# Window attention scores from stacked operand halves, in a two-layer hybrid backbone kernel

## Chip, cores and metric

The kernel runs on one core of a Trainium2 chip. The metric is the device time of one execution in microseconds (us), lower is better; the median of 3 runs is quoted.

## What is computed

The reference is a two-layer backbone over 256 context tokens and 256 latent tokens (width 1024). Each layer mixes tokens with three branches, a state space model (s5), latent attention (MLA) and windowed attention with a sink, merges them with gates and an output projection, and then runs a 16-expert feed-forward (MoE). The part that matters here is the windowed branch: 8 query heads and 2 key heads of 64 channels.

```python
def axial_rope(x, row, col):            # cos, sin from row and column angles
    x1, x2 = x[..., : d // 2], x[..., d // 2:]
    return jnp.concatenate([x1 * cos - x2 * sin, x1 * sin + x2 * cos], axis=-1)

def window_branch(qc, kc, vc, ql, kl, vl, sink, row, col, update_ctx):
    ...
    qb = axial_rope(q, row, col).reshape(B, nb, BLOCK, WIN_KV_HEADS, WIN_GROUP, WIN_HEAD_DIM)
    k_rot = axial_rope(kl.reshape(B, L, WIN_KV_HEADS, WIN_HEAD_DIM), row, col)
    ...
    s_band = jnp.einsum('bnqkgd,bnskd->bnkgqs', qb, kb).astype(jnp.float32) * WIN_SCALE
    s_band = jnp.where(valid[None, :, None, None], s_band, NEG_INF)
    s_ctx = jnp.einsum('bnqkgd,bskd->bnkgqs', qpb, kc).astype(jnp.float32) * WIN_SCALE
    p = jax.nn.softmax(jnp.concatenate([s_band, s_ctx, sk], axis=-1), axis=-1)
```

Latent queries attend to rotated latent keys within 128 positions and, without rotation, to all context keys. In layer 0 context queries attend to context keys as well.

## The kernel before

Products that need float32 accuracy are done in float32r, a format that TensorE takes in one pass. A value is split in two float32r parts, high (the rounded value) and low (the rest). `put` (L433) makes both, with one ScalarE copy for the high part and one VectorE subtraction for the low one. `mm3` (L438) multiplies two such pairs in three passes: high by high, high by low, low by high. A product of plain float32 operands is one call of `mm` too, and shows as two matmul records in the trace.

`win_proj` (L1230) makes the operands of the windowed branch. First come the keys of both heads (projection, `rope` of the latent half, parts into KW), then four query tiles f, each with two heads on 128 rows: 24 passes of projection, `put` of the plain queries into QP, and `rope` into QR. `rope` (L1240) swaps the halves of each head with a permutation matmul (`permr`), multiplies by cosine and sine on VectorE (L1249, L1250), adds on GpSimd (L1251) and splits the result with `put`. The key's permutation is in plain float32, the queries' in two float32r passes over the parts.

`win_branch` (L1278) then walks over four head pairs hp and two query tiles qt. For each of the two heads a, one PSUM tile `sc` takes three passes with the context keys (L1297), three with the latent keys (L1299) and the mask as one pass with the identity (L1302). The operands stand on the 64 rows of one head, so each of these passes uses 64 of TensorE's 128 rows; only the mask uses 128. That is six passes and a mask per softmax row block, 16 such groups in a layer. In layer 0 there are eight more groups, of context queries on context keys: six passes and no mask (L1312). `softmax` (L1051) reads the tile on VectorE and ScalarE, `attend` (L1077) transposes the weights and multiplies them with the values. `sc` has two PSUM buffers.

Between the groups `tick` (L203) issues filler work: the branch projection of the s5 branch (`branches`, passes of F<-extra,wc over 128 rows), and in layer 0 also the modulation products (`ada_group`, records ad<-arena,silu_c, which use 32 columns of the array at a time). A scheduler sets the final order of each engine. Names in the profile: sc<-big,big and sc<-big are the score passes, sc<-round is the mask, F and mm are projections, wc are split weights, tp are transposes.

Of the kernel before, what the change touches and what calls it, by code (L numbers as in the profile page):

```python
# [7 lines left out]
F32 = mybir.dt.float32  # L8
# [37 lines left out]
def _constants():  # L46
# [28 lines left out]
    _ROUND.append(np.concatenate([pm, np.where(k <= q, 0.0, big)], 1).astype(np.float32))  # L75
# [86 lines left out]
class Net:  # L162
# [1067 lines left out]
    def win_proj(self, l, h, full):  # L1230
# [5 lines left out]
        parts = lambda i, o, f, n: self.bg[i][:, o:o + 2 * f * n].rearrange("p (f r n) -> p f r n", f=f, r=2)  # L1236
        QP, QR, KW = parts(0, 0, 4, NQ), parts(1, 0, 4, 256), parts(1, 2048, 2, 512)
        kf = self.buf("wkf", 512)

        def rope(dst, src, two=None):  # L1240
            pp = self.ps("sc")
            if two is None:
                self.mm(pp[:, :256], self.permr.bitcast(F32), src, True, True)
            else:
                for r in range(2):
                    self.mm(pp[:, :256], self.permr, two[:, r], r == 0, r == 1)
# [4 lines left out]
            nc.gpsimd.tensor_tensor(dst if two is None else t1, t1, t2, op=OP.add)  # L1251
            if two is not None:
                self.put(dst, t1)
# [9 lines left out]
        rope(kf[:, 256:512], kp[:, 256:512])  # L1263
        for kv in range(2):
            own, other = [slice(64 * a, 64 * a + 64) for a in (kv, 1 - kv)]
            self.put(KW[own, kv], kf[own])
            self.copy(KW[other, kv], KW[own, kv].bitcast(F32), "a" if kv else "v")
        for f in range(4):
# [4 lines left out]
            self.put(QP[:, f], pt[:, q0:])  # L1273
            rope(QR[:, f], pt[:, 256:], QP[:, f, :, 256 - q0:])
# [3 lines left out]
    def win_branch(self, l, Z, QP, QR, KW, full, tick):  # L1278
# [6 lines left out]
        two = lambda t, c: (t[:, 0, c], t[:, 1, c])  # L1285
        pv = lambda t: t.rearrange("p (a n) -> p a n", a=2)
        for hp in range(4):
# [3 lines left out]
            for qt in range(2):  # L1291
# [435 lines left out]
    def build(self, layers=(0, 1), stop=None):  # L1727
# [3 lines left out]
        with tc.tile_pool(name="main", bufs=1) as main, \  # L1731
# [11 lines left out]
            self.round = main.tile([128, 384], F32R, name="round")  # L1743
# [282 lines left out]
```

## Time and profile before

| what | us |
|---|---|
| median of 3 runs | 2080.92 (2080.52 to 2082.33) |
| the profiled execution | 2081.91 |
| its span | 2080.1 |
| TensorE matmul busy | 1800.9 (87%) |
| VectorE busy | 1030.1 (50%) |
| ScalarE busy | 603.5 (29%) |
| GpSimd busy | 444.6 (21%) |

The window stage runs twice: projection at about 282 to 310 us and branch at 310 to 400 us in layer 0, and 1386 to 1401 and 1401 to 1456 us in layer 1. A record of a matmul has a duration that includes its way through the array, so neighbours overlap in time; what a pass takes is read from the distance between starts. "Busy" of TensorE is therefore near full wherever passes follow each other, also where each starts late.

### The profile page before, as it was taken

To read this page: it belongs to the slowest core of one execution; us is meant where nothing else is said; L and a number is where in the kernel's file an instruction comes from. 1 tells how busy PE (TensorE), PEld (TensorE's weight loads), DVE (VectorE), ACT (ScalarE), POOL (GpSimd) and SP (SyncE) were. 2 spreads that over 40 slices of the span, in tenths; PEclk is the share of its full clock that TensorE was granted. 3 is DMA by queue.
4 is the path that set the end of the run, shared out by engine and by line. 5 is a ranking of instruction groups with operands and counts; after the bars stand their busy time and mean duration, and the time that the engine had idled before them with its cause. 6 is when DMAs were issued, how large, how long until landed. Compare 5 with 4: busy or idle time off the path is not lost.

```text
span 2080.1 us, 31699 instructions
## 1 busy us (share of the span) xinstructions
PE 1800.9 (87%) x12421; PEld 1116.5 (54%) x12421; DVE 1030.1 (50%) x2433; ACT 603.5 (29%) x1354; POOL 444.6 (21%) x590
## 2 busy tenths in 40 slices
PE   7898999999998699999799979999998876676665
PEld 5866566677776534334233358887886532232222
DVE  6867656656537712323465276977767321010102
ACT  3354343444433321000111075354553100000000
POOL 4745420011135100001334034640114000000000
PEclk9999999999999899999999989998999887686867
DMA  9256736222237689999999813541367799999996
GB/s 348 80 158 226 245 120 200 92 71 72 63 132 264 262 332 421 421 422 415 417 415 349 335 47 99 155 121 51 103 216 301 282 421 421 421 421 422 420 421 279
DMA packets 173013, 543.88 MB, mean 261 GB/s; under 512 B 18752, under 2 KB 101952, under 8 KB 122688
## 3 DMA queue, kind: packets, MB, share of 16 engines
q1 hardware_dynamic: 172864, 541.86, 68.4%
q8 instruction: 98, 1.61, 0.3%
q14 instruction: 51, 0.42, 0.1%
HBM read 540.77 MB, written 1.05 MB: 260 GB/s over the span
## 4 chain that ended last, share of the span: by engine, by line
PE 55%; DMA 25%; DVE 14%; issue 2%; ACT 2%; POOL 2%; SPq 0%; POOLq 0%; DVEq 0%; ACTq 0%
PE sc L247 17%; PE mm L247 16%; PE F L247 13%; DMA arena<-in_w_down 5%; PE ad L247 4%; PE tp L250 4%; DMA arena<-in_w_up 4%; DMA arena<-in_w_gate 3%; DVE wc L431 2%; DVE arena L572 2%; DMA big<-in_w_gate 2%; DMA h<-in_w_gate 2%; DMA arena<-in_w_in 2%; DMA arena<-in_w_ada 2%; DVE arena L885 1%
## 5 line engine op out<-in xcount | busy, mean ns | idle before, releaser
L247 PE MATMUL F<-h,wc 128*128 128x256 f32 (+1 forms) x1200 | 233.3, 345 | 2.0 <-DVE wc L431 2.0
L247 PE MATMUL sc<-arena,xs 128*32 128x256 f32 (+1 forms) x1336 | 190.4, 528 | 40.1 <-DMA arena<-in_w_up 23.3
L428 ACT ACTIVATE wc<-arena 128x512 fp32r<-128x512 f32 (+2 forms) x280 | 170.6, 619 | 180.6 <-PE F L247 63.7
L250 PE MATMUL tp<-const,arena 128*128 128x128 f32 (+2 forms) x815 | 141.7, 297 | 79.1 <-DVE arena L291 12.2
L247 PEld LDWEIGHTS F<-h,wc 128*128 128x128 f32 x1200 | 185.8, 191 | 33.2 <-issue 6.2
L247 PE MATMUL mm<-arena 128*32 128x256 f32 (+5 forms) x1244 | 186.8, 462 | 17.3 <-DMA arena<-in_w_down 10.0
L431 DVE TENSOR_TENSOR wc<-arena,wc 128x512 fp32r<-128x512 f32 (+2 forms) x205 | 158.9, 787 | 84.6 <-ACT wc L428 84.0
L431 POOL TENSOR_TENSOR wc<-arena,wc 128x512 fp32r<-128x512 f32 (+2 forms) x75 | 98.1, 1307 | 382.6 <-ACT wc L428 340.3
L1678 DVE TENSOR_TENSOR arena<-mm,arena 32x512 f32<-32x512 f32 (+1 forms) x128 | 70.9, 554 | 217.4 <-PE mm L247 215.9
L250 PEld LDWEIGHTS tp<-const,arena 128*128 128x128 f32 (+2 forms) x815 | 97.8, 149 | 145.0 <-issue 35.6
L242 ACT ACTIVATE arena<-tp 128x512 f32<-128x512 f32 (+3 forms) x142 | 62.1, 463 | 346.3 <-PE tp L250 301.9
L247 PEld LDWEIGHTS sc<-arena,xs 128*32 128x32 f32 (+1 forms) x1336 | 61.1, 132 | 144.7 <-issue 76.7
L247 PEld LDWEIGHTS mm<-arena 128*32 128x32 f32 (+2 forms) x1244 | 76.8, 137 | 102.0 <-issue 51.9
L247 PE MATMUL sc<-h,xs 128*32 128x256 f32 (+1 forms) x752 | 110.8, 526 | 19.9 <-DMA h<-in_w_gate 11.2
L264 POOL TENSOR_TENSOR lnq<-lnq,k 128x1 f32<-128x1 f32 x22 | 14.4, 658 | 501.4 <-DVE lnq L311 471.1
L1655 DVE TENSOR_TENSOR arena<-arena,sc 128x512 f32<-128x512 f32 (+1 forms) x32 | 17.8, 555 | 181.3 <-PE sc L247 181.0
L247 PE MATMUL sc<-big,xs 128*32 128x256 f32 (+1 forms) x632 | 86.0, 525 | 23.8 <-DMA big<-in_w_up 12.7
L1653 ACT ACTIVATE arena<-sc 128x512 f32<-128x512 f32 (+1 forms) x32 | 15.7, 491 | 290.9 <-PE sc L247 290.9
L247 PE MATMUL mm<-wc,h 128*128 128x512 f32 (+2 forms) x288 | 81.3, 406 | 6.2 <-DVE wc L431 2.8
L247 PE MATMUL F<-extra,wc 128*128 128x256 f32 (+1 forms) x432 | 83.4, 337 | 3.1 <-DVE smst L1060 2.1
L1654 DVE SCALAR_TENSOR_TENSOR arena<-arena,sc 128x512 f32<-128x512 f32 (+1 forms) x32 | 17.7, 554 | 135.3 <-ACT arena L1653 135.2
L247 PEld LDWEIGHTS sc<-h,xs 128*32 128x32 f32 (+1 forms) x752 | 36.7, 132 | 87.2 <-issue 60.5
(366 smaller groups left out, 3165.4 us busy)
## 6 DMA issues: line engine op xcount, KB each, us to landing
arena<-in_w_up SPq DMA_DIRECT2D x65, 1024.0 KB, 16.6
arena<-in_w_down SPq DMA_DIRECT2D x61, 1024.0 KB, 19.8
arena<-in_w_gate SPq DMA_DIRECT2D x48, 1024.0 KB, 19.5
h<-in_w_gate SPq DMA_DIRECT2D x41, 1024.0 KB, 13.9
arena<-in_w_ada SPq DMA_DIRECT2D x80, 512.0 KB, 5.8
arena<-in_w_in SPq DMA_DIRECT2D x66, 512.0 KB, 3.9
big<-in_w_up SPq DMA_DIRECT2D x26, 1024.0 KB, 19.8
h<-in_w_down SPq DMA_DIRECT2D x26, 1024.0 KB, 18.5
```

The costliest lines, as they stand in the source:

```text
L242: self.nc.scalar.activation(out, in_, AF.Copy)
L247: return self.nc.tensor.matmul(out, lhsT, rhs, start=start, stop=stop, skip_group_check=True)
L250: self.nc.tensor.transpose(out, in_, self.c("idn")[:n, :n])
L264: self.nc.gpsimd.tensor_tensor(out, in_, e.to_broadcast(list(in_.shape)), op=OP.pow)
L428: nc.scalar.activation(hi, src, AF.Copy)
L431: eng.tensor_tensor(lo, src, hi.bitcast(F32), op=OP.subtract)
L572: tt = lambda o, a, b, op: keep[0](v.tensor_tensor(o, a, b, op=op))
L885: v.tensor_tensor_scan(z, rb, z, 0.0, op0=OP.mult, op1=OP.add)
L1653: nc.scalar.activation(th, gu[0][:, :NF], AF.Tanh, scale=0.5)
L1654: v.scalar_tensor_tensor(th, th, 1.0, gu[0][:, :NF], op0=OP.add, op1=OP.mult)
L1655: v.tensor_tensor(th, th, gu[1][:, :NF], op=OP.mult)
L1678: v.tensor_tensor(YS[n][o:o + 32, c * NF:(c + 1) * NF], yp[r:r + 32, :NF], m5[r:r + 32], op=OP.mult)
```

## The change

The scores take two passes per product in place of three. The first, high by high, is as before over the 64 rows of the head. The second is over all 128 rows: for the queries of head a the high part stands on the head's own 64 rows and the low part on the other 64, and the keys are laid out the other way round, so that one pass adds high by low and low by high.

- `put_heads` replaces `put` for queries: for each of the two heads one ScalarE copy and one VectorE subtraction over 64 rows, the latter with its result on the other 64 rows.
- KW is laid out so that the copy to the other head's rows reverses the parts (same number of operations).
- `rope` can no longer use split parts. The permutation is done in plain float32, on each 64-row half by itself (64x64 products), for keys and queries. A ScalarE copy brings the query tile from PSUM to `kp` first. `permr` is a 64-column constant.

```diff
+        def put_heads(dst, src):
+            for a in range(2):
+                nc.scalar.activation(dst[rows[a], a], src[rows[a]], AF.Copy)
+                v.tensor_tensor(dst[rows[1 - a], a], src[rows[a]], dst[rows[a], a].bitcast(F32), op=OP.subtract)
...
-        def rope(dst, src, two=None):
+        def rope(dst, src, two=True):
             pp = self.ps("sc")
-            if two is None:
-                self.mm(pp[:, :256], self.permr.bitcast(F32), src, True, True)
-            else:
-                for r in range(2):
-                    self.mm(pp[:, :256], self.permr, two[:, r], r == 0, r == 1)
+            for r in rows:
+                self.mm(pp[r, :256], self.permr[r].bitcast(F32), src[r], True, True)
...
-            if two is not None:
-                self.put(dst, t1)
+            if two:
+                put_heads(dst, t1)
...
-            self.put(KW[own, kv], kf[own])
-            self.copy(KW[other, kv], KW[own, kv].bitcast(F32), "a" if kv else "v")
+            hi, lo = KW[own, kv, 1 - kv], KW[own, kv, kv]
+            nc.scalar.activation(hi, kf[own], AF.Copy)
+            v.tensor_tensor(lo, kf[own], hi.bitcast(F32), op=OP.subtract)
+            self.copy(KW[other, kv], KW[own, kv, ::-1].bitcast(F32), "a" if kv else "v")
...
-            self.put(QP[:, f], pt[:, q0:])
-            rope(QR[:, f], pt[:, 256:], QP[:, f, :, 256 - q0:])
+            put_heads(QP[:, f], pt[:, q0:])
+            self.copy(kp[:, 0:256], pt[:, 256:], "a")
+            rope(QR[:, f], kp[:, 0:256])
...
+        def score(out, q, k, a, qc, kc, stop):
+            self.mm(out, q[rows[a], a, qc], k[rows[a], 1 - a, kc], True, False)
+            self.mm(out, q[:, a, qc], k[:, a, kc], False, stop)
...
-                    self.mm3(sc[a][:, 0:256], two(QP[rows[a], hp], qc), two(KW[rows[a], kv], slice(0, 256)), True, True)
+                    score(sc[a][:, 0:256], QP[:, hp], KW[:, kv], a, qc, slice(0, 256), True)
...
-                    self.mm3(sc[a][:, 256:512], two(QR[rows[a], hp], qs), two(KW[rows[a], kv], slice(256, 512)),
-                             True, False)
+                    score(sc[a][:, 256:512], QR[:, hp], KW[:, kv], a, qs, slice(256, 512), False)
...
-                        self.mm3(sc[a][:, qt], two(QP[rows[a], hp], slice(qt * 128, qt * 128 + 128)),
-                                 two(KW[rows[a], kv], slice(0, 256)), True, True)
+                        score(sc[a][:, qt], QP[:, hp], KW[:, kv], a, slice(qt * 128, qt * 128 + 128), slice(0, 256), True)
```

TensorE's order in the first score groups of layer 0. The number after a name tells the tile apart; each sc is the score tile of one head, the size is output rows by columns. Before:

```order
L247 MATMUL sc_2718<-big_2418,big_2417 128x256 x3
L247 MATMUL sc_2718<-big_2418 128x256 x3
L247 MATMUL sc_2718<-round 128x128
L247 MATMUL sc_2794<-big_2418,big_2417 128x256 x3
L247 MATMUL sc_2794<-big_2418 128x256 x3
L247 MATMUL sc_2794<-round 128x128
L247 MATMUL ad_2396<-arena,silu_c 32x256
```

The same groups on TensorE in the changed kernel:

```order
L247 MATMUL sc_2739<-big_2418,big_2417 128x256 x2
L247 MATMUL sc_2739<-big_2418 128x256 x2
L247 MATMUL sc_2739<-round 128x128
L247 MATMUL ad_2396<-arena,silu_c 32x256 x4
L247 MATMUL sc_2811<-big_2418,big_2417 128x256 x2
L247 MATMUL sc_2811<-big_2418 128x256 x2
L247 MATMUL sc_2811<-round 128x128
L247 MATMUL ad_2396<-arena,silu_c 32x256 x4
```

Each x2 is one pass over 64 rows and one over 128, in place of three over 64. The modulation products also lie in other places between the groups.

TensorE's order around the rotation of a query tile in layer 0's projection, before:

```order
L247 MATMUL sc_2499<-big_2417,round 128x256
L247 MATMUL mm_2549<-h_229,wc 128x512
L247 MATMUL mm_2549<-h_230,wc 128x512
L247 MATMUL mm_2549<-h_229,wc 128x512 x2
L247 MATMUL sc_2499<-big_2417,round 128x256
```

and in the changed kernel:

```order
L247 MATMUL mm_2560<-h_229,wc 128x512 x2
L247 MATMUL sc_2503<-arena,round 64x256 x2
L247 MATMUL mm_2560<-h_230,wc 128x512
```

Two 128-row passes over the parts, apart from each other, have become two 64x64 products that stand together and read the copy in the arena.

VectorE's order in layer 1's projection, between two splits of weights (wc), before:

```order
L431 TENSOR_TENSOR wc<-arena,wc 128x512
L1250 TENSOR_TENSOR arena<-sc_10276,const 128x256
L436 TENSOR_TENSOR big_10153<-mm_10284,big_10153 128x256
L1249 TENSOR_TENSOR arena<-mm_10284,const 128x256
L436 TENSOR_TENSOR big_10154<-arena,big_10154 128x256
L431 TENSOR_TENSOR wc<-arena,wc 128x512
```

and in the changed kernel (L1244 is the subtraction in `put_heads`, L1253 and L1254 are the products with cosine and sine):

```order
L431 TENSOR_TENSOR wc<-arena,wc 128x512
L1254 TENSOR_TENSOR arena<-sc_10211,const 128x256
L1244 TENSOR_TENSOR big_10126<-mm_10268,big_10126 64x256
L1244 TENSOR_TENSOR big_10126<-F_10221,big_10126 64x256
L1244 TENSOR_TENSOR big_10126<-mm_10268,big_10126 64x256
L1244 TENSOR_TENSOR big_10127<-arena,big_10127 64x256 x2
L1253 TENSOR_TENSOR arena<-arena,const 128x256
L1254 TENSOR_TENSOR arena<-sc_10258,const 128x256
L1253 TENSOR_TENSOR arena<-arena,const 128x256
L1244 TENSOR_TENSOR big_10127<-arena,big_10127 64x256 x2
L431 TENSOR_TENSOR wc<-arena,wc 128x512
```

Over the whole projection of a layer the 8 subtractions over 128 rows have become 16 over 64 rows.

## Rows read from the trace of the kernel before

**Rows 1.** Busy time of each engine, share of the span, instructions (page, part 1).

```profile
PE 1800.9 (87%) x12421; PEld 1116.5 (54%) x12421; DVE 1030.1 (50%) x2433; ACT 603.5 (29%) x1354; POOL 444.6 (21%) x590
```

**Rows 2.** Busy time by stretch: projection, branch, slow clock; layer 0, then 1.

```profile
core 0: us, PE busy (x) PEld busy (x) DVE busy (x) ACT busy (x) POOL busy (x), PEclk, DMA share, GB/s
282.00:310.00 28.00, 28.00 (x145) 21.24 (x145) 18.60 (x43) 15.72 (x36) 12.18 (x15) 1.00 0.22 66
310.00:398.00 88.00, 86.57 (x587) 56.52 (x587) 60.25 (x192) 32.44 (x99) 4.98 (x4) 1.00 0.55 177
398.00:405.00 7.00, 7.00 (x21) 4.90 (x22) 5.68 (x31) 3.50 (x14) 0.00 (x0) 0.51 0.02 4
1386.00:1400.00 14.00, 13.82 (x109) 13.19 (x107) 13.63 (x34) 10.62 (x20) 6.63 (x6) 1.00 0.36 114
1400.00:1436.00 36.00, 34.49 (x243) 28.45 (x244) 31.17 (x99) 18.38 (x50) 6.06 (x6) 1.00 0.29 89
1436.00:1456.00 20.00, 16.92 (x66) 11.35 (x64) 10.82 (x43) 6.05 (x20) 0.00 (x0) 0.58 0.00 0
```

**Rows 3.** Chain of waits, 282 to 396 us: its shares by line.

```profile
by line: PE F L247 27.9%; PE mm L247 20.9%; PE sc L247 20.5%; PE ad L247 14.1%; PE tp L250 11.2%; DMA arena<-in_w_ada 5.3%; DVE smst L1062 0.6%; issue 0.1%
```

**Rows 4.** Chain of waits in layer 1, pieces in time: start, length, what.

```profile
1397.48 1.09 DVE wc L431
...
1398.85 0.41 DVE big L436
...
1400.03 1.14 DVE wc L431
...
1411.16 1.47 PE F L247 x12
1412.63 1.16 PE sc L247 x7
```

**Rows 5.** Groups of instructions: name, shape, count; busy us, mean ns; idle before.

```profile
L247 PE MATMUL sc<-big,big 64*128 64x256 f32 x144 | 29.2, 324 | 2.8 <-ACT arena L1069 1.8 <-DVE arena L1250 1.0
L247 PE MATMUL sc<-big 64*128 64x256 f32 x96 | 18.0, 295 | 0.0
```

**Rows 6.** Timeline of TensorE, two score groups: start, length, tile, count.

```profile
315.60 0.62 PE L247 MATMUL sc<-big,big 64*128 64x256 f32 x3
316.06 0.52 PE L247 MATMUL sc<-big 64*128 64x256 f32 x3
316.50 0.33 PE L247 MATMUL sc<-round 128*128 128x128 f32 x1
316.76 0.62 PE L247 MATMUL sc<-big,big 64*128 64x256 f32 x3
```

**Rows 7.** Timeline of TensorE, layer 1's projection, passes of one shape.

```profile
1392.99 1.12 PE L247 MATMUL mm<-h,wc 128*128 128x256 f32 x8
1393.95 0.28 PE L247 MATMUL sc<-big,round 128*128 128x256 f32 x1
```

**Rows 8.** Instructions on the tile round: min/median/max ns, first and last start.

```profile
L247 PE MATMUL sc<-big,round x16: 276/283/385, 295.9 to 1402.6; 128*128 128x256 f32 x16
L247 PE MATMUL sc<-arena,round x4: 379/380/483, 282.5 to 1389.8; 128*128 128x256 f32 x4
```

**Rows 9.** Timeline of TensorE, a run of 64x64 float32 products in the s5 stage.

```profile
226.12 1.96 PE L247 MATMUL sc<-arena,big 64*64 64x128 f32 x32
228.01 0.64 PE L247 MATMUL ad<-arena,silu_c 128*32 128x256 f32 x8
```

**Rows 10.** Groups of instructions: splits over 64 and over 128 rows.

```profile
L436 DVE TENSOR_TENSOR big<-mm,big 64x512 fp32r<-64x512 f32 x16 | 11.0, 687 | 11.0 <-ACT big L435 10.8
L436 DVE TENSOR_TENSOR big<-mm,big 128x512 fp32r<-128x512 f32 x10 | 6.9, 688 | 6.7 <-ACT big L435 6.6
L436 DVE TENSOR_TENSOR big<-arena,big 128x256 fp32r<-128x256 f32 x24 | 10.8, 456 | 1.2 <-ACT big L435 1.2
L435 ACT ACTIVATE big<-arena 128x256 fp32r<-128x256 f32 x24 | 9.8, 411 | 6.3 <-POOL arena L1251 3.8 <-DVE arena L1182 2.4
```

**Rows 11.** Timeline of TensorE, the end of layer 1's window branch.

```profile
1438.73 0.77 PE L247 MATMUL sc<-big,big 64*128 64x256 f32 x3 [1.84 <-ACT arena L1069]
...
1440.48 1.01 PE L247 MATMUL sc<-big,big 64*128 64x256 f32 x3
...
1443.78 1.54 PE L250 MATMUL tp<-const,arena 128*128 128x128 f32 x6 [1.25 <-DVE arena L1075]
```

More of the change, by code (lines that the diff above doesn't have):

```diff
@@ L73, in _constants @@
     big = np.float32(-1e30 / WIN_SCALE)
-    _ROUND.append(np.concatenate([pm, np.where(k <= q, 0.0, big)], 1).astype(np.float32))
+    _ROUND.append(np.concatenate([pm[:, 0:64] + pm[:, 64:128], np.where(k <= q, 0.0, big)], 1).astype(np.float32))
     parts["iota"] = np.tile(np.arange(1, 33, dtype=np.float32), (128, 1))
@@ L1237, in win_proj @@
         QP, QR, KW = parts(0, 0, 4, NQ), parts(1, 0, 4, 256), parts(1, 2048, 2, 512)
+        rows = [slice(0, 64), slice(64, 128)]
+        def put_heads(dst, src):
+            for a in range(2):
+                nc.scalar.activation(dst[rows[a], a], src[rows[a]], AF.Copy)
+                v.tensor_tensor(dst[rows[1 - a], a], src[rows[a]], dst[rows[a], a].bitcast(F32), op=OP.subtract)
         kf = self.buf("wkf", 512)
-        def rope(dst, src, two=None):
+        def rope(dst, src, two=True):
             pp = self.ps("sc")
-            if two is None:
-                self.mm(pp[:, :256], self.permr.bitcast(F32), src, True, True)
-            else:
-                for r in range(2):
-                    self.mm(pp[:, :256], self.permr, two[:, r], r == 0, r == 1)
+            for r in rows:
+                self.mm(pp[r, :256], self.permr[r].bitcast(F32), src[r], True, True)
             t1 = self.buf("wr1", 256)
@@ L1250, in rope @@
             v.tensor_tensor(t2, pp[:, :256], self.c("wsin"), op=OP.mult)
-            nc.gpsimd.tensor_tensor(dst if two is None else t1, t1, t2, op=OP.add)
-            if two is not None:
-                self.put(dst, t1)
+            nc.gpsimd.tensor_tensor(t1 if two else dst, t1, t2, op=OP.add)
+            if two:
+                put_heads(dst, t1)
             self.free("wr1", "wr2")
@@ L1262, in win_proj @@
         v.tensor_copy(kf[:, 0:256], kp[:, 0:256])
-        rope(kf[:, 256:512], kp[:, 256:512])
+        rope(kf[:, 256:512], kp[:, 256:512], False)
         for kv in range(2):
             own, other = [slice(64 * a, 64 * a + 64) for a in (kv, 1 - kv)]
-            self.put(KW[own, kv], kf[own])
-            self.copy(KW[other, kv], KW[own, kv].bitcast(F32), "a" if kv else "v")
+            hi, lo = KW[own, kv, 1 - kv], KW[own, kv, kv]
+            nc.scalar.activation(hi, kf[own], AF.Copy)
+            v.tensor_tensor(lo, kf[own], hi.bitcast(F32), op=OP.subtract)
+            self.copy(KW[other, kv], KW[own, kv, ::-1].bitcast(F32), "a" if kv else "v")
         for f in range(4):
@@ L1742, in build @@
             self.const = main.tile([128, NCONST], F32, name="const")
-            self.round = main.tile([128, 384], F32R, name="round")
-            self.idnr, self.permr, self.maskr = [self.round[:, 128 * i:128 * i + 128] for i in range(3)]
+            self.round = main.tile([128, 320], F32R, name="round")
+            self.idnr, self.permr, self.maskr = self.round[:, 0:128], self.round[:, 128:192], self.round[:, 192:320]
             arena = main.tile([128, self.ARENA_COLS], F32, name="arena")
@@ L1806, in layer @@
                 self.load(self.const[:, 128:], self.ins["const"][:, 128:])
-                self.load(self.buf("round", 256), self.ins["round"])
+                self.load(self.buf("round", 192), self.ins["round"])
             h = self.modulated_split(l, x, [full or t < 2 for t in range(4)], step, self.stats)
```

3 lines of the change are left out of this document (1 added, 2 removed).

## The prediction

> **What bounds the kernel now.** I read the busy times first: TensorE is busy for 87% of the span, no other engine for more than 50% [rows 1]. The change lies in four stretches, so the stretches come next [rows 2]. In layer 0's projection TensorE is busy for all 28.00 us, in its window branch for 86.57 of 88 us, and VectorE for two thirds. The chain of waits says the same: from 282 to 396 us it is TensorE on every line but two small ones, a weight load for the modulation (5.3%) and a VectorE line (0.6%) [rows 3]. So in layer 0 a microsecond more or less on TensorE is a microsecond of the kernel, since the filler has to be issued anyway and the expert stage only starts behind it. Layer 1 differs in two places. In its projection VectorE is busy for 13.63 of 14 us [rows 2], and the chain runs over VectorE's weight splits and part splits [rows 4]; VectorE bounds it, with TensorE close behind. At the end of its window branch (1436 to 1456 us) TensorE waits for softmax, 1.84 and 1.25 us at a time [rows 11], at a granted clock of 0.58 [rows 2]. In between (1400 to 1436) TensorE is busy for 34.49 of 36 us and the chain alternates between filler and scores on it [rows 4].
>
> **Removed: 80 score passes.** There are 144 + 96 = 240 passes over 64 rows [rows 5]; a third goes. What one takes is read from starts, not from the 295 to 324 ns of its record: eight passes of the same 256 columns over 128 rows take 1393.95 - 1392.99 = 0.96 us, 0.12 us each [rows 7]. In a score group the second triple follows the first after 0.46 us and the mask follows that after 0.44 us [rows 6], so a pass over 64 rows is no shorter than one over 128, but also hardly longer than 0.12. 80 x 0.12 = 9.6 us fewer.
>
> **Added: changes between 64 and 128 rows.** A whole group, six passes of 64 rows and a mask over 128, takes 316.76 - 315.60 = 1.16 us from its start to the next group's [rows 6]. Seven passes at 0.12 make 0.84. The 0.32 left are two changes of height, one into the mask and one out of it; no engine is waited for there. Layer 1 gives a second reading: 12 filler passes over 128 rows and a group take 1.47 + 1.16 = 2.63 us [rows 4], 19 passes at 0.12 make 2.28, and 0.35 is left for one change there and back. A lone pass of 256 columns between two of 64 rows streams twice the columns of the mask, and can hide less of its weight load; half a pass, 0.06, on top of 0.35 is my upper end. I take 0.37 per change there and back, with 0.32 and 0.41 as ends.
>
> In the new code each group runs 64, 128, 64, 128 rows and then the mask; before it ran 64 six times and then the mask. That is one change there and back more for each of 40 groups (16 and 8 in layer 0, 16 in layer 1). Counted along the two orders, TensorE enters 64-row passes 41 times before and 80 times after, so 39 more. 39 x 0.37 = 14.4 us (12.5 to 16.0). Scores together: 14.4 - 9.6 = 4.8 us more (2.9 to 6.4).
>
> **Rope on TensorE.** Sixteen float32r passes go [rows 8], 0.12 each, eight in a layer. In their place each query tile gets two 64x64 products in plain float32, two records each, as the four records of the two key products show [rows 8]. In the s5 stage 32 records of 64x64 products with 128 columns take 1.89 us [rows 9]; less a change of about 0.15 that is 0.11 for two records side by side. With 256 columns that is 0.22, and 0.44 for both products if the two halves run side by side; one after the other it would be 0.87. The Trainium skill, "TensorEngine Tiling (Array Packing)", section "Key Properties", says that tiles work independently and that a change of the tiling mode, but not of the tile, drains TensorE. The s5 rows agree with its first half; by it a rope costs 0.44 and one change, without it 0.87. That the two halves need only one change, into and out of 64 rows, I take from the s5 run too, which has 32 records in one piece. Layer 0: 4 x 0.44 - 8 x 0.12 = 0.8, and five changes at 0.37 (four queries, one key) = 1.85; together 2.6 us (4.3 if the halves run in turn). The key's product takes as long as before: four records there were, and two pairs side by side come to the same.
>
> **Splits on VectorE and ScalarE.** A subtraction over 64 rows takes 687 ns for 512 columns, over 128 rows 688: rows are free [rows 10]. So `put_heads` doubles the time of `put`. In layer 1, 8 more subtractions of 256 columns at 0.41 us (0.456 in the mean, 0.41 where GpSimd is quiet, as in [rows 4]) are 3.3 us more on VectorE. It is the bound of that projection, so I count them in full, and count the rope's 2 to 3 us on TensorE there as covered by it. Its lower end is 1.0 (VectorE work for MLA that is not yet needed slips behind), its upper end 5.0: the query copy adds a step of 0.41 on ScalarE before each rope, and the last rope stands in front of the first score group. ScalarE gets 12 more copies of 0.41 to 0.6 in a layer; it is busy for 10.62 of 14 us [rows 2], and what I give it is in that upper end. In layer 0, VectorE has 9 us free in 28 and gets some 4.4 more: nothing there, while TensorE's 28 us cover it.
>
> **Order.** Along layer 0's new order TensorE visits the modulation products 31 times in place of 25, a shape change each. At the same 0.37 that is 2.2 us; the ends are 0 and 2.5. In the last 20 us of layer 1's branch TensorE waits for softmax, and some of its groups' extra time is hidden: 1.0 us off (0 to 1.5).
>
> **Sum.** 4.8 + 2.6 + 3.3 + 2.2 - 1.0 = 11.9 us more on the profiled execution, whose 2081.91 become 2093.8. It lies 1.0 above the median, so I forecast 2093. With all low ends it is 2.9 + 2.4 + 1.0 + 0 - 1.5 = 4.8, with all high ends 6.4 + 4.3 + 5.0 + 2.5 = 18.2: 2086 to 2099.
>
> **Rivals.** (a) Height is free between passes, and what I read as two changes is something of the mask alone. Then the passes saved are all that counts: -9.6 + 0.8 + 3.3 = -5.5, a median of 2075, faster. It decides once a change there and back costs under 5.5 / 50 = 0.11 us, over the 50 that I counted. Against it: the filler's readings in layer 1 give the same 0.35 as the mask's in layer 0 [rows 4, 6]. Chance 0.12. (b) VectorE's softmax paces the branch, so that neither passes nor changes show, and only layer 1's projection grows: 2080.9 + 3.3 = 2084, no difference to be measured. For it: VectorE is busy for 31.17 of 36 us [rows 2], and the waits of [rows 11]. Against it: the chain [rows 3]. Chance 0.13. (c) The clock. It fell to half after TensorE had waited, at 398 and in 1436 to 1456 us [rows 2]. A score group takes 1.75 us there, 1438.73 to 1440.48 [rows 11], in place of 1.16. A stretch of 7 us at half clock thus costs some 2.4 us. With more pauses in the passes three more such stretches would give 2093 + 7 = 2100. Chance 0.15. (d) That the change doesn't do what it says, the two heights being gathered into longer runs by the scheduler, its order rules out.
>
> **How the numbers follow.** My forecast has 0.60. A measurement of this kernel tells apart about 0.2%, 4.2 us: under 2076.8 is faster, over 2085.1 slower. (a) is faster, (b) is the same, the forecast and (c) are slower: 0.12, 0.13, 0.75. The range leaves out (a) and a little of (b) below, and of (c) above: 2080 to 2103.
>
> **What would show it.** In the new profile, 160 score passes, half of them over 64 rows; a group from its start to the next should take about 1.16 + 0.37 - 0.24 = 1.29 us and not 0.92. Each rope should show two pairs of 64x64 records that start together. Layer 1's projection should grow by about 3 us with VectorE on the chain. From 310 us to the end of layer 0's branch the stretch should be longer by about 5 us, layer 1's branch by about 1 to 2. I am wrong if a lone 128-row pass between 64-row ones starts and ends within 0.25 us, or if the stretches behind the branches change.

## The result, and the profile after

The changed kernel takes 2111.38 us (median of 4 runs, 2107.24 to 2112.79) beside 2080.72 (4 runs) for the kernel before. The medians differ by 30.7 us. The estimated ratio is 1.0136, with an interval of [1.0124, 1.0148], which stands for 28 us. The profiled execution has a span of 2108.4 us against 2080.1, which is 28.3 more. So the kernel is slower by about 28 us where 12 were forecast, and lies above the range.

The changed kernel's busy times (page, part 1; columns as in [rows 1]):

```profile
PE 1813.2 (86%) x12361; PEld 1113.2 (53%) x12361; DVE 1037.7 (49%) x2449; ACT 612.1 (29%) x1378; POOL 443.1 (21%) x590
```

TensorE has 60 records fewer and is busy for 12 us more, VectorE for 8 and ScalarE for 9 more. That explains less than half. The stages (us) tell more. I measure four of them by TensorE's records: a projection from the key's rope to the first score pass, a branch from there to the last mask.

| kernel | projection 0 | branch 0 | projection 1 | branch 1 |
|---|---|---|---|---|
| before | 27.5 | 85.5 | 12.0 | 50.2 |
| after | 33.3 | 90.9 | 24.0 | 53.4 |
| difference | +5.8 | +5.4 | +12.0 | +3.2 |

These add up to 26.4 of the 28.3 us. Busy time by stretch in the changed kernel, to set beside [rows 2]: layer 0's projection, its first score groups, the end of its branch, then layer 1's projection in two pieces, its branch, and the branch's end:

```profile
core 0: us, PE busy (x) PEld busy (x) DVE busy (x) ACT busy (x) POOL busy (x), PEclk, DMA share, GB/s
282.00:315.00 33.00, 30.91 (x178) 21.16 (x176) 24.61 (x52) 20.88 (x47) 12.48 (x15) 1.00 0.38 119
315.00:322.00 7.00, 7.00 (x20) 4.91 (x19) 2.76 (x9) 1.70 (x5) 0.72 (x1) 0.52 0.80 269
410.00:418.00 8.00, 8.00 (x27) 5.52 (x25) 5.38 (x26) 3.28 (x13) 0.00 (x0) 0.57 0.01 1
1402.00:1414.00 12.00, 7.92 (x63) 6.79 (x61) 11.66 (x21) 8.46 (x18) 4.66 (x5) 1.00 0.43 131
1414.00:1432.00 18.00, 13.43 (x55) 9.98 (x55) 10.03 (x24) 6.90 (x18) 3.28 (x4) 0.62 0.20 60
1432.00:1468.00 36.00, 35.44 (x211) 26.07 (x212) 28.21 (x94) 15.72 (x45) 3.92 (x3) 1.00 0.19 59
1468.00:1487.00 19.00, 17.00 (x59) 10.12 (x58) 9.09 (x39) 6.83 (x20) 0.73 (x1) 0.55 0.00 0
```

TensorE was busy for 13.82 of 14 us in layer 1's projection before [rows 2]; now it idles for a third of the first 12 us, and after that it runs at a mean granted clock of 0.62. The clock also falls at 315 us, where [rows 2] has 1.00 from 310 to 398.

**Layer 1's projection.** Waits of TensorE from 1402 to 1427 us (line waited for: total, times, longest):

```profile
PE sc L247 <- ACT arena L242: 8.7, 2, 5.2
```

`sc` is the rope's permutation, L242 the new copy to `kp`. What delays the copy is in the timeline of ScalarE, VectorE and TensorE for the last query tile, whose projection F ends at 1422.24 (start, length, engine, line, tile, and in brackets the idle time before and what ended it):

```profile
1422.29 0.38 ACT L1243 ACTIVATE big<-F 64x256 fp32r<-64x256 f32 x1 [2.56 <-PE F L247]
1422.57 0.62 ACT L428 ACTIVATE wc<-arena 128x512 fp32r<-128x512 f32 x1
1422.69 0.42 DVE L1244 TENSOR_TENSOR big<-F,big 64x256 fp32r<-64x256 f32 x1 [0.65 <-ACT big L1243]
1423.09 0.84 ACT L1243 ACTIVATE big<-arena 64x256 fp32r<-64x256 f32 x2
1423.22 0.69 DVE L431 TENSOR_TENSOR wc<-arena,wc 128x512 fp32r<-128x512 f32 x1
1423.94 0.87 DVE L1244 TENSOR_TENSOR big<-arena,big 64x256 fp32r<-64x256 f32 x2
1423.95 0.38 ACT L1243 ACTIVATE big<-F 64x256 fp32r<-64x256 f32 x1
1424.84 0.42 DVE L1244 TENSOR_TENSOR big<-F,big 64x256 fp32r<-64x256 f32 x1
1425.30 0.38 ACT L242 ACTIVATE arena<-F 128x256 f32<-128x256 f32 x1 [0.97 <-DVE big L1244]
1425.74 1.12 PE L247 MATMUL sc<-arena,round 64*64 64x256 f32 x4 [3.49 <-ACT arena L242]
```

Five operations read the PSUM tile F, and they take turns: ScalarE, VectorE, ScalarE, VectorE, ScalarE. Each starts only after the one before, and between the turns both engines do what stands ahead in their own queues (a weight split, the other tile's rope parts). The copy is the fifth, and the rope waits for it. At the end ScalarE stands idle for 0.97 us with nothing but the copy to do, released by VectorE's subtraction, though both only read F. So the waits in the program order two reads of this tile like a read and a write. The same splits of the rope's result, which read SBUF (`big<-arena`), take no turns: at 1423.09 and 1423.94 two ScalarE copies and two VectorE subtractions each run in one piece. From F's end to the rope it takes 3.5 us; for an earlier tile TensorE waits 5.16 us, until 1415.08.

**Layer 0's projection and first scores.** TensorE's timeline in the changed kernel:

```profile
311.10 1.07 PE L247 MATMUL ad<-arena,silu_c 128*32 128x256 f32 x16
314.26 0.64 PE L247 MATMUL ad<-arena,silu_c 128*32 128x256 f32 x8 [2.09 <-DMA arena<-in_w_ada]
314.83 0.71 PE L247 MATMUL sc<-arena,round 64*64 64x256 f32 x4
315.47 1.09 PE L247 MATMUL sc<-big,big 64*128 64x256 f32 x2
316.49 1.09 PE L247 MATMUL sc<-big 64*128 64x256 f32 x2
317.38 0.31 PE L247 MATMUL sc<-round 128*128 128x128 f32 x1
317.48 5.13 PE L247 MATMUL F<-extra,wc 128*128 128x512 f32 x12
322.54 0.64 PE L247 MATMUL ad<-arena,silu_c 128*32 128x256 f32 x8
323.11 0.70 PE L247 MATMUL sc<-big,big 64*128 64x256 f32 x2
323.74 0.70 PE L247 MATMUL sc<-big 64*128 64x256 f32 x2
324.27 0.22 PE L247 MATMUL sc<-round 128*128 128x128 f32 x1
324.42 0.64 PE L247 MATMUL ad<-arena,silu_c 128*32 128x256 f32 x8
```

Modulation products have moved ahead of the last rope and of the first score group, and there they meet weights that have not landed: 2.09 us of waiting. At half clock the group at 315.47 then takes 2.01 us and 12 filler passes 5.06. At full clock a group takes 324.42 - 323.11 = 1.31 us; the forecast was 1.29. The modulation products that moved ahead are work as well: the projection now holds 52 of their records and held 30 before, and the branch holds 160 in place of 184.

The groups of instructions with 64-row score passes confirm the counts, 48 + 32 = 80, where [rows 5] has 240:

```profile
L247 PE MATMUL sc<-big,big 64*128 64x256 f32 x48 | 19.5, 406 | 0.0
L247 PE MATMUL sc<-big 64*128 64x256 f32 x32 | 13.2, 412 | 0.0
```

### The profile page after: what moved, and what is told of

Read it like the earlier page. It is cut to its first block, busy times and chain, and to the rows that moved or that the text cites. A ratio compares the mean times of both kernels' runs of the same rounds, so it can differ in the third digit from the quotient of the medians.

```text
span 2108.4 us, 31619 instructions
## 1 busy us (share of the span) xinstructions
PE 1813.2 (86%) x12361; PEld 1113.2 (53%) x12361; DVE 1037.7 (49%) x2449; ACT 612.1 (29%) x1378; POOL 443.1 (21%) x590
## 3 DMA queue, kind: packets, MB, share of 16 engines
HBM read 540.74 MB, written 1.05 MB: 257 GB/s over the span
## 4 chain that ended last, share of the span: by engine, by line
PE 57%; DMA 21%; DVE 15%; issue 2%; ACT 2%; POOL 2%; SPq 0%; POOLq 0%; DVEq 0%; ACTq 0%
PE sc L247 19%; PE mm L247 16%; PE F L247 13%; PE ad L247 5%; PE tp L250 4%; DMA arena<-in_w_down 4%; DMA arena<-in_w_up 3%; DVE wc L431 2%; DVE arena L572 2%; DMA big<-in_w_up 2%; DMA arena<-in_w_gate 2%; DMA big<-in_w_gate 2%; DMA h<-in_w_gate 2%; DMA big<-in_w_down 2%; DVE arena L885 2%
## 5 line engine op out<-in xcount | busy, mean ns | idle before, releaser
L250 PE MATMUL tp<-const,arena 128*128 128x128 f32 (+2 forms) x815 | 140.3, 296 | 80.4 <-DVE arena L291 11.9
L242 ACT ACTIVATE arena<-tp 128x512 f32<-128x512 f32 (+3 forms) x142 | 62.1, 463 | 338.4 <-PE tp L250 294.0
L247 PE MATMUL mm<-wc,h 128*128 128x512 f32 (+2 forms) x288 | 80.9, 406 | 6.8 <-DVE wc L431 3.1
## 6 DMA issues: line engine op xcount, KB each, us to landing
arena<-in_w_down SPq DMA_DIRECT2D x61, 1024.0 KB, 19.8
big<-in_w_up SPq DMA_DIRECT2D x26, 1024.0 KB, 19.8
h<-in_w_down SPq DMA_DIRECT2D x26, 1024.0 KB, 18.2
```

Of the source, the lines that this page charges most:

```text
L242: self.nc.scalar.activation(out, in_, AF.Copy)
L247: return self.nc.tensor.matmul(out, lhsT, rhs, start=start, stop=stop, skip_group_check=True)
L250: self.nc.tensor.transpose(out, in_, self.c("idn")[:n, :n])
```

## The experiments

Four theories were at stake. **P** (in later runs **Q**): the rope waits for a copy that stands last in the queue for one PSUM tile. **V**: the doubled splits keep VectorE busy for longer. **H**: changes of height cost what was forecast. **B**: the branches are longer only because the projections deliver late. Single runs have a rival of their own (N, G, D), told in their expectation. Three of the kernels, projection_only, scores_only and half_splits, do not lay the operands out as their scores want them, so only their time is read. Some expectations count layer 1's projection from the first pass of its query tiles, some 3 us ahead of the key's rope, where the tables here begin. Stages of all runs in us, from one profile each:

| kernel | time | ratio to before, interval | proj. 0 | branch 0 | proj. 1 | branch 1 |
|---|---|---|---|---|---|---|
| after | 2111.38 | 1.0136 [1.0124, 1.0148] | 33.3 | 90.9 | 24.0 | 53.4 |
| copy_first | 2095.33 | 1.0077 [1.0058, 1.0096] | 29.6 | 89.7 | 20.0 | 48.5 |
| from_sbuf | 2104.15 | 1.0109 [1.0092, 1.0126] | 29.3 | 86.9 | 19.8 | 57.6 |
| tall | 2080.56 | 0.9999 [0.9989, 1.0008] | 33.0 | 74.7 | 23.9 | 41.4 |
| tall_copy_first | 2079.59 | 0.9998 [0.9988, 1.0007] | 29.6 | 76.0 | 19.8 | 44.2 |
| projection_only | 2098.54 | 1.0080 [1.0061, 1.0099] | 34.1 | 88.7 | 23.9 | 48.5 |
| scores_only | 2091.79 | 1.0044 [1.0031, 1.0057] | 27.5 | 89.2 | 12.0 | 52.5 |
| stacked_rope | 2113.80 | 1.0151 [1.0134, 1.0168] | 32.3 | 94.3 | 18.2 | 54.3 |
| tall_stacked_rope | 2073.26 | 0.9957 [0.9942, 0.9971] | 32.5 | 77.5 | 18.2 | 42.0 |
| half_splits | 2094.48 | 1.0066 [1.0051, 1.0081] | 28.8 | 92.6 | 14.2 | 50.4 |
| tall_sr_pool | 2074.66 | 0.9966 [0.9953, 0.9979] | 33.8 | 74.2 | 17.4 | 40.5 |
| tall_dma | 2073.18 | 0.9968 [0.9955, 0.9982] | 28.5 | 80.9 | 11.3 | 45.5 |
| mixed | 2070.90 | 0.9949 [0.9931, 0.9967] | 31.9 | 76.1 | 11.3 | 46.3 |

### One half of the change at a time

Before's projection with the new scores (scores_only), and the new projection with before's three-pass scores (projection_only):

```diff
# projection_only: win_branch as before, here the context keys
...
-                    score(sc[a][:, 0:256], QP[:, hp], KW[:, kv], a, qc, slice(0, 256), True)
+                    self.mm3(sc[a][:, 0:256], two(QP[rows[a], hp], qc), two(KW[rows[a], kv], slice(0, 256)), True, True)
...
# scores_only: win_proj as before, and the same lines the other way round
```

> The changed projection with the three-pass scores of the kernel before; the operands are not laid out for those scores, so what is added up is not the reference's scores, and only the time is read. Theory Q (the lost time has two parts that do not depend on each other: the queue for the projection tile in PSUM, +5.8 us in layer 0's projection and +12.0 in layer 1's, and the changes of height in the branches, +5.4 and +3.2): projections 32 to 34 and 23 to 25 us, branches near those of the kernel before, 85 to 87 and 49 to 52, time 2096 to 2102. Rival B (the branches are longer because the projections deliver late): branches stay at 89 to 92 and 52 to 55, time 2105 to 2112.

> The projection of the kernel before with the two-pass scores of the changed kernel; the operands are not laid out for them, so the scores are not the reference's, and only the time is read. Theory Q: projections as before, 27 to 29 and 12 to 13 us, branches 89 to 92 and 52 to 55, time 2086 to 2092: what 39 changes of height at 0.37 less 80 passes at 0.12 forecast, 4.8, or some more. Rival B: branches as before, 85 to 87 and 49 to 52, time 2077 to 2083.

Measured: 0.8% slower with the projection alone, 16.6 us, and 0.44% with the scores alone, 9.2 us. Together that is 25.8, close to the 28.3 of the whole change. Both times lie in Q's ranges. Each stage shows its own part: in scores_only the projections are 27.5 and 12.0 as before and the branches 3.7 and 2.3 longer; in projection_only the projections are like after's. Layer 1's branch is not longer there (48.5), which speaks against B; layer 0's is, by 3.2, above Q's 85 to 87 and just under B's 89 to 92. It begins like after's with a stretch at a low clock (0.62 from 316 to 325 us) behind a wait for modulation weights.

### The copy first

copy_first moves one line: the copy to `kp` ahead of the four operations of `put_heads`. from_sbuf goes further: the copy takes the whole tile and everything else reads the copy, so that PSUM has one reader.

```diff
 # copy_first
-            put_heads(QP[:, f], pt[:, q0:])
             self.copy(kp[:, 0:256], pt[:, 256:], "a")
+            put_heads(QP[:, f], pt[:, q0:])
             rope(QR[:, f], kp[:, 0:256])
 # from_sbuf
-            put_heads(QP[:, f], pt[:, q0:])
-            self.copy(kp[:, 0:256], pt[:, 256:], "a")
-            rope(QR[:, f], kp[:, 0:256])
+            self.copy(kp[:, 0:NQ], pt[:, q0:], "a")
+            put_heads(QP[:, f], kp[:, 0:NQ])
+            rope(QR[:, f], kp[:, 256 - q0:NQ])
```

> One line of the changed kernel is moved: the ScalarE copy of the query tile for the rotation stands before put_heads and not behind it. The work is the same. Theory P (the rotation waits for a copy that is last in a row of five steps on one PSUM bank, ScalarE, VectorE, ScalarE, VectorE, ScalarE, each behind other work in its queue): layer 1's projection, from the first query tile's first pass to the first score pass, falls from 27.1 us to 15 to 20, and the median from 2111 to 2097 to 2104. Rival V (VectorE has more to do than the stretch has time for, whatever the order): the stretch stays over 24 us and the median within 3 us of 2111.

> The changed kernel with the whole query tile copied to SBUF first; both the splits and the rotation read the copy. The number of splits stays. Theory P: no alternation on the PSUM bank is left, so layer 1's projection takes 15 to 20 us in place of 27.1, the median 2097 to 2104; where it is worse than the kernel that only moves the copy, the single copy buffer is what waits. Rival V: over 24 us, median within 3 us of 2111.

copy_first takes 2095.33: 16 us less than after by the medians and the profiled executions, 12 by the ratios (1.0136 and 1.0077). So about half of the loss hung on the place of one copy. But neither theory's ranges were met. Counted from the first pass of the query tiles, layer 1's projection takes 23.0 us in copy_first and 22.8 in from_sbuf, in place of 27.1. That is above P's 15 to 20 and below V's 24. Both times lie just outside P's 2097 to 2104, and far from V's 2111. The queue is a part of the cause, not all of it. Of the 16 us only 4.0 lie in layer 1's projection, 3.7 in layer 0's, 4.9 in layer 1's branch and 1.2 in layer 0's; the rest lies outside these stages. Waits of TensorE in copy_first, 1399.9 to 1421 us:

```profile
PE sc L247 <- ACT arena L242: 3.4, 2, 2.8
PE F L247 <- DVE big L1244: 2.0, 1, 2.0
```

The wait for the copy falls from 8.7 to 3.4 us, and a new one appears: the PSUM tile F comes free only after the last subtraction. Busy times of the same stretch (columns as above):

```profile
1399.90:1421.00 21.10, 15.74 (x97) 12.76 (x97) 19.05 (x35) 13.02 (x28) 7.97 (x8) 0.84 0.32 101
```

VectorE is busy for 19.05 of 21.1 us. from_sbuf has the same projections (29.3 and 19.8) without those readers, so with the queue for the PSUM tile gone the stage is no shorter. Its layer 1 branch is longest of all, 57.6. The trace shows it at the lower clock for the first 18 us (columns as above):

```profile
1412.00:1420.00 8.00, 7.49 (x25) 5.50 (x24) 5.46 (x14) 2.05 (x5) 2.07 (x2) 0.50 0.19 66
1420.00:1430.00 10.00, 10.00 (x36) 8.12 (x36) 4.08 (x16) 2.37 (x9) 0.16 (x1) 0.50 0.17 53
```

Why the clock stayed low for so long there is open.

### Half the splits, and the rope from the parts

half_splits is copy_first with one split over 128 rows, as before, in place of two over 64. stacked_rope is the changed kernel with its rope taken from the stacked parts, in two float32r products over 128 rows, and no copy for the queries.

```diff
 # half_splits: put_heads is
-            for a in range(2):
-                nc.scalar.activation(dst[rows[a], a], src[rows[a]], AF.Copy)
-                v.tensor_tensor(dst[rows[1 - a], a], src[rows[a]], dst[rows[a], a].bitcast(F32), op=OP.subtract)
+            self.put(dst, src)
 # stacked_rope: permr holds the 64-column permutation twice
-            self.copy(kp[:, 0:256], pt[:, 256:], "a")
-            rope(QR[:, f], kp[:, 0:256])
+            rope(QR[:, f], pt[:, 256:], QP[:, f, :, 256 - q0:])
 ...
+                self.mm(pp[:, :256], self.permr, two[:, 1], True, True)
+                self.mm(pp[rows[0], :256], self.permr[:, 0:64], two[:, 0], True, True)
```

> The run with the copy moved ahead, but with one split over 128 rows (one ScalarE copy, one VectorE subtraction) in place of two over 64 for queries and rope: half as many split operations on both engines, the same 64x64 ropes from the same copy, the same two-pass scores. The high and low parts do not land where those scores want them, so the output is not the reference's and only the time is read. Theory V (the doubled splits make layer 1's projection long by VectorE's volume, 8 subtractions at 0.41 to 0.7 us, once the queue for the copy is out of the way): layer 1's projection 14 to 16 us in place of 20.0, its branch no longer than 51, time 2086 to 2091. Theory Q (only the queue for the projection tile counts, and the copy is already first in it): layer 1's projection stays at 19 to 21, time 2092 to 2098. Layer 0's projection: 28 to 30 by both.

> The changed kernel with its rope taken from the stacked high and low parts, two float32r products over 128 rows, in place of a plain copy of the queries and two 64x64 float32 products; the doubled splits stay, four operations for a query tile and four for its rope. Theory Q (the rope's plain copy, fifth in the queue for the projection tile, is what TensorE waits for): layer 0's projection 28 to 31 us, layer 1's 15 to 19, time 2098 to 2104. Rival V (the doubled splits themselves, VectorE's volume, make the projections long): layer 1's projection stays at 21 to 25, time 2106 to 2112.

half_splits: layer 1's projection falls from 20.0 to 14.2 us, as V said. TensorE's waits from 1399.3 to 1414 us:

```profile
PE F L247 <- DVE big L436: 1.5, 1, 1.5
PE sc L247 <- ACT arena L242: 0.5, 1, 0.5
```

and the busy times:

```profile
1399.30:1414.00 14.70, 12.71 (x95) 10.11 (x94) 14.57 (x26) 9.60 (x20) 7.81 (x7) 1.00 0.39 124
```

VectorE is busy for 14.57 of 14.7 us and bounds the stage, at full clock. The run also has fewer readers of the PSUM tile, but from_sbuf, with one reader and doubled splits, stays at 19.8, so the shorter queue can hardly be the reason. Both theories hold in part in that stage: of its 12.0 us, 4.0 go with the place of the copy, 5.8 with the doubled splits, and 2.2 remain. V missed the time, though: 2094.48, which is what Q said, and not 2086 to 2091. The branches take back 2.9 and 1.9, and the rest lies behind them.

stacked_rope: layer 1's projection falls from 24.0 to 18.2, inside Q's 15 to 19, layer 0's only to 32.3 (Q: 28 to 31), and the whole kernel is no faster than after (2113.80). TensorE's waits there, 1407.2 to 1426 us:

```profile
PE sc L247 <- DVE big L1244: 5.8, 2, 3.4
```

With the copy gone, the rope waits for the fourth operation of the same queue. Both forecasts for the total failed, Q's 2098 to 2104 and V's 2106 to 2112. Branch 0 is longer (94.3; its first 7 us come after 3.0 us of waiting for modulation weights and have a mean clock of 0.65 from 314 to 322 us) and branch 1 too (54.3). That these give back what the projection gained is read from the sums; no run shows why.

### All score passes over 128 rows

tall runs the first score pass over all 128 rows too. That adds low by low, and no pass of a score group changes height any more. tall_copy_first does both.

```diff
-            self.mm(out, q[rows[a], a, qc], k[rows[a], 1 - a, kc], True, False)
+            self.mm(out, q[:, a, qc], k[:, 1 - a, kc], True, False)
```

> The changed kernel with the first score pass over all 128 rows too (it then adds low by low, a fourth term), so that no pass of a score group changes the height. As many passes as in the changed kernel. Theory H (a change of height there and back costs 0.37 us or a little more): a warm group from its first pass to the next group goes from 1.31 us to 0.6 to 0.7, 40 groups, some hidden at the end of layer 1: the median falls by 20 to 28 us to 2083 to 2091. Rival N (the passes themselves are slow, because of the stacked operands or the PSUM bank): groups stay over 1.1 us and the median within 4 us of 2111. Layer 1's projection stays at 27 us by both.

> Both edits, the moved copy and the first pass over 128 rows. If theories P and H hold and their costs lie one behind the other: 2070 to 2080, faster than the kernel before. If one hides the other: over 2085.

tall is faster than after by 28 us (ratios) to 31 us (medians), with the same number of passes, and equal to the kernel before. H had forecast 20 to 28. TensorE's timeline in tall, one group and what follows it:

```profile
321.99 0.51 PE L247 MATMUL sc<-big,big 128*128 128x256 f32 x2
322.33 0.40 PE L247 MATMUL sc<-big 128*128 128x256 f32 x2
322.57 0.22 PE L247 MATMUL sc<-round 128*128 128x128 f32 x1
322.72 0.64 PE L247 MATMUL ad<-arena,silu_c 128*32 128x256 f32 x8
```

A group takes 322.72 - 321.99 = 0.73 us, in place of 1.31. The 0.58 between them is too little for two changes of height there and back: these groups stand between modulation products of 32 columns, and in tall their first pass and their mask are spaced wider than the same passes beside filler (0.34 and 0.15 us to the next start, against 0.23 and 0.06). The price shows where both kernels have the same full-height neighbours, 12 filler passes ahead of the group and a transpose behind it. In layer 1 of the changed kernel:

```profile
1442.51 1.68 PE L247 MATMUL F<-extra,wc 128*128 128x256 f32 x12
1444.12 0.70 PE L247 MATMUL sc<-big,big 64*128 64x256 f32 x2
1444.74 0.70 PE L247 MATMUL sc<-big 64*128 64x256 f32 x2
1445.28 0.23 PE L247 MATMUL sc<-round 128*128 128x128 f32 x1
1445.34 0.29 PE L250 MATMUL tp<-const,arena 128*128 128x128 f32 x1
```

and in tall:

```profile
1424.30 1.69 PE L247 MATMUL F<-extra,wc 128*128 128x256 f32 x12
1425.83 0.40 PE L247 MATMUL sc<-big,big 128*128 128x256 f32 x2
1426.06 0.40 PE L247 MATMUL sc<-big 128*128 128x256 f32 x2
1426.30 0.23 PE L247 MATMUL sc<-round 128*128 128x128 f32 x1
1426.36 0.29 PE L250 MATMUL tp<-const,arena 128*128 128x128 f32 x1
```

From the first filler pass to the transpose that is 1445.34 - 1442.51 = 2.83 us and 1426.36 - 1424.30 = 2.06. The 0.77 between them are two changes there and back, 0.39 each, near the 0.37 of the forecast. Two passes in tall take 1426.06 - 1425.83 = 0.23, which is 0.12 each, again as forecast. At 0.58 to 0.77 for each of 40 groups the changes of height make 23 to 31 us, and the branches are shorter by 16.2 and 12.0, so these changes are enough to account for the gain. A smaller part in layer 0 may be the clock: tall stays at 1.00 through its stage, after has the stretch at 315. With the copy first as well, nothing more is gained, and the hope of a kernel faster than before (2070 to 2080) failed: tall_copy_first takes 2079.59 at a ratio of 0.9998. The projections fall by 3.4 and 4.1, the branches grow by 1.3 and 2.8.

### Versions that beat both

tall_stacked_rope takes both rope and first pass over 128 rows. tall_sr_pool adds the rope's subtractions on GpSimd. tall_dma keeps before's single splits and before's rope, and DMA brings the parts to their stacked places. mixed takes layer 0 from tall_stacked_rope and layer 1 from tall_dma.

```diff
 # tall_dma
+            self.put(SP_[f % 2], pt[:, q0:])
+            rope(SR_[f % 2], pt[:, 256:], SP_[f % 2][:, :, 256 - q0:])
+            stack(QP[:, f], SP_[f % 2])
+            stack(QR[:, f], SR_[f % 2])
 # stack: for each head a, parts 0 and 1 of its rows
+                nc.sync.dma_start(dst[rows[a], a].bitcast(F32), parts[rows[a], 0].bitcast(F32))
+                nc.sync.dma_start(dst[rows[1 - a], a].bitcast(F32), parts[rows[a], 1].bitcast(F32))
```

> The same rope, and the first score pass over 128 rows too, so that nothing in a query tile or a score group changes height (the low by low term is added). If the gains of the two edits add up: branches 73 to 76 and 40 to 44 us, projections as with the rope alone, time 2064 to 2074. If, as with the copy moved ahead, what the projection gains is given back in the branch: 2077 to 2082.

> The run with all score passes and ropes over 128 rows, with the rope's subtractions on GpSimd in place of VectorE. Theory V: VectorE loses 8 subtractions in each projection, layer 1's projection 15 to 17 us in place of 18.2, time 2067 to 2072. Rival G (GpSimd is slower for one and stretches VectorE's operations while it runs): layer 1's projection 18 to 21, time 2073 to 2078.

> Ropes and splits exactly as in the kernel before (one copy and one subtraction over 128 rows, rope in two float32r products from the parts), and the parts are then brought to their stacked places by DMA, four transfers of 64 rows for each split; all score passes over 128 rows. Theory V: with the splits single again the projections are as before, 27 to 29 and 12 to 14 us, and the branches as in the run with all passes over 128 rows, 75 to 78 and 41 to 45, time 2057 to 2066. Rival D (the transfers stand in SyncE's queue ahead of the weights and wait there for VectorE, so weights come late): layer 0's branch 80 or more, layer 1's projection 15 or more, time 2070 to 2085.

> Layer 0 as in the run with all score passes and ropes over 128 rows (parts split into their stacked places by VectorE and ScalarE), layer 1 as in the run that stacks them by DMA after single splits. If a layer keeps what it showed alone: layer 0's projection 32 to 34 and branch 74 to 78 us, layer 1's projection 11 to 13 and branch 43 to 46, time 2064 to 2071. If what one stage gains is given back by the filler that moves behind it: 2072 to 2078, no faster than either.

All four are faster than the kernel before, by 0.3 to 0.5%. tall_stacked_rope's time lies inside its additive forecast, with branch 0 a little above it (77.5 for 73 to 76). tall_sr_pool is no better: its projection is 17.4, between V's 15 to 17 and G's 18 to 21, its time is G's, and TensorE still waits for VectorE's part of the queue (6.6 us). In tall_dma layer 1's projection is 11.3, shorter than before the change, but the time is in D's range (2070 to 2085) and not in V's 2057 to 2066. Busy times of that projection:

```profile
1388.00:1400.00 12.00, 11.22 (x87) 10.51 (x85) 11.53 (x22) 8.37 (x16) 7.40 (x7) 1.00 0.62 189
```

VectorE has its old work again, and TensorE is busy for 11.22 of 12 us. Layer 0's branch is longer, 80.9 beside 74.7 in tall, which is D's number but not clearly its reason: TensorE waits 1.2 us for weights there and 2.7 for a softmax. mixed is the fastest median, 2070.90, at the upper end of its forecast; its interval overlaps those of the other three, so that it beats the kernel before but not certainly them.

## Why the prediction was wrong

**Right: the counts and prices of the score groups; luck in their sum.** A group of 1.31 us was forecast as 1.29, a change there and back is 0.39 where 0.37 was taken, and a pass is 0.12, in the comparison of the changed kernel with tall. With the measured prices, one change more and two passes fewer in each of 40 groups, that is 40 x (0.39 - 0.24) = 6.0 us, 3.6 in layer 0 and 2.4 in layer 1, and scores_only's branches are longer by 3.7 and 2.3. The terms *Removed*, *Added*, *Order* and its last subtraction also add up to 4.8 + 2.2 - 1.0 = 6.0, but by luck. scores_only visits the modulation products 20 times, the kernel before 19 times, so *Order* had next to nothing to cost there, and in layer 1 the groups' price shows in full, so the 1.0 hidden behind softmax does not show. What the changed kernel's six more visits (25) cost, no run isolates. The whole of scores_only lost 9.2 us (6.5 to 11.9 by its interval). In its profile most of the rest lies behind layer 0's branch.

**Right: the rope's two halves.** Four 64x64 records start at 310.52 in the changed kernel and the next work at 311.10: 0.58 us in all, against 0.87 had they run in turn. That agrees with what the prediction drew from the Trainium skill, "TensorEngine Tiling (Array Packing)", section "Key Properties": tiles are independent, and a change of the tiling mode drains. On TensorE itself the rope costs no more than forecast.

**Wrong: *Splits on VectorE and ScalarE*.** This term had +3.3 for layer 1's projection, with 5.0 as its upper end, and nothing for layer 0. Layer 1's projection grew by 12.0. The step that failed was to count the splits as volume on VectorE and the copy as "a step of 0.41 on ScalarE before each rope". I had costed each of five operations by its length, on its own engine, and not asked in which order they may touch the tile that they all read. They take turns, so the copy's price is the sum of five steps and of all that stands between them on two queues: 8.7 us of waiting, where the kernel before has 1.4. Behind the waits TensorE works at the lower clock: the 20 passes from 1416.13 to 1420.69 take 4.56 us, at 0.12 each they would take 2.4, and the three ropes from 1415.08 on take 1.05, 0.81 and 1.04 us in place of 0.58. I estimate 3.3 us of the 12.0 for that. Moving the copy recovers 12 to 16 us of the whole kernel, and 4.0 us in this stage. The volume itself was sized right, 8 more subtractions of 0.42 us; what it costs was not: halving the splits gives back 5.8 us in this stage, not 3.3, and the stage then runs at 1.00 in place of 0.84.

**Wrong: layer 0 at "nothing".** VectorE does have room there, 24.61 of 33 us. The rope's term gave this projection 2.6 us, and it is longer by 5.8. Of that 2.09 are the wait for modulation weights. *Order* had counted what visits to the modulation products cost in shape changes; that they come earlier than their weights was not asked. Some 1.6 us more are moved work: 22 more modulation records, at 324.99 - 324.42 = 0.57 us for eight. The branch is rid of about as many, and is still longer by 5.4, since to the 3.6 us for height come 2.9 us at the lower clock (12 filler passes 5.06 for 2.90, a group 2.01 for 1.31). These are estimates from single stretches. copy_first waits 1.0 us for the weights and half_splits not at all, and their projections are 29.6 and 28.8. The rest I did not separate.

**The rivals.** (a) is excluded: height costs 0.39, well over 0.11. (b) is excluded: the branches did grow. (c) came true beside the main cause. It gave 7 us to three more stretches at half clock. Before had them at 398 and from 1436, the changed kernel has them at 315, 410, 1414, 1424 and from 1469, three more. From starts at either clock I estimate their price at 2.9 us at 315 and 5.3 at 1414 and 1424 (the 3.3 above, a group 2.01 for 1.22, 12 filler passes 2.76 for 1.61), 8.2 in all. Two of the new ones begin in or behind the rope's waits and one behind the wait for modulation weights, but such a wait is not enough for it: tall waits 1.87 us for the same weights at the same place and stays at 1.00. In half_splits, where the rope's waits in layer 1 are 0.5 us, the projection runs at 1.00. By these estimates the score groups have 6.0, the longer waits in both projections 9.2 and the clock 8.2 of the 26.4 us that the four stages lost; the ropes' own time on TensorE lies in the rest. What is left open is why gains in a projection are so often given back in the branch behind it, and why the stretch from the last mask to the expert stage in layer 0 varies between 330.6 and 337.6 us over these profiles.

## What to carry to other kernels

When an edit adds readers to a PSUM tile, do not price them one by one: write down in which order the engines may read it, and count the whole row up to the reader for which TensorE waits. Putting that reader first gave 12 to 16 us here, though nothing on top of tall. Where a pass gets wider or narrower than its neighbours, compare the whole group from start to start, with and without the change of height, between neighbours of the same shape: padding a pass to the height of its neighbours was worth about 30 us here, though it computes more. A stage that gains can lose again in the next one, so the total decides, and not the stage.

## What the runs showed of the hardware

- A pass over 64 rows between passes over 128 costs 0.39 us for the change there and back (0.77 us per group with two of them, 2.83 against 2.06 with 12 filler passes ahead). Between products of 32 columns the same group differs by 0.58 (1.31 against 0.73). The full-height pass that replaces it takes 0.12 us like the others of 256 columns.
- A ScalarE read of a PSUM tile stood still for 0.97 us until a VectorE read of the same tile was over. These are the waits of the program; whether the two engines could read side by side was not tried.
- After waits of 2.09 and 5.16 us the granted clock was 0.52 and 0.62 in the stretches shown, the lower of its two levels (1.2 and 2.4 GHz) for most of them. At that level 12 filler passes of 512 columns took 322.54 - 317.48 = 5.06 us, in place of 314.15 - 311.25 = 2.90 in the kernel before (starts from its timeline), whose clock was 1.00 there [rows 2]. After a wait of 1.87 us in tall, for the same weights, the clock stayed at 1.00.
- DMA between places in SBUF carried 8 splits of four transfers each without a longer layer 1 projection (11.3 us), on a queue that also brings weights.
